# Gates by seven products and sums by accumulating transfers in a two-layer decoder trunk

## The chip, the cores and the metric

The kernel runs on one core of a Trainium2 chip. The metric is the device time of one execution in microseconds (us), the median of three runs. A core has five engines with a queue each: TensorE (PE), VectorE (DVE), ScalarE (ACT), GpSimd (POOL) and SyncE (SP, which here only issues transfers). DMA engines move data between HBM and the on-chip memory SBUF; matrix products are summed in PSUM banks of 128x512 fp32.

## The reference

One sequence of 256 tokens of width 1024 passes two layers. Layer 0 mixes tokens by gated linear attention (GLA), layer 1 by block attention (with 256 tokens this is plain causal attention). What the change touches is the output gate g of the GLA mixer and the feed-forward part (SwiGLU, hidden width 2816):

```python
def gla_mixer(x, w_in, w_gk, b_gk, norm_g, w_out):
    q, k, v, g, gk_low = split_cols(x @ w_in, GLA_COLS)
    ...
    o = chunk_gla(q, to_heads(k, GLA_HEADS), to_heads(v, GLA_HEADS), to_heads(log_a, GLA_HEADS))
    o = from_heads(rms_norm(o.astype(x.dtype), norm_g)) * jax.nn.silu(g)
    return o @ w_out

def swiglu_ffn(x, w_gu, w_down):
    gate, up = jnp.split(x @ w_gu, 2, axis=-1)
    return (jax.nn.silu(gate) * up) @ w_down
...
        x = layer_norm(DEEPNORM_ALPHA * x + y, ln_g[i, 0], ln_b[i, 0])
        x = layer_norm(DEEPNORM_ALPHA * x + swiglu_ffn(x, w_gu, w_down), ln_g[i, 1], ln_b[i, 1])
```

## The kernel before

**Precision.** Every fp32 operand of a large product is held as a high part (an ACT cast to fp32r, "h" at the end of its name) and a low part (a DVE subtraction, "l"). A product of 128 rows of contraction is three matmuls: high x high, low x high, high x low (`mm3`, lines 301 to 303; in the seven products lines 557, 559 and 560). A weight tile is 256 rows x 512 columns, loaded by SP as one raw tile of 128x1024 (512 KB), and split once into h and l (lines 265 and 266, in the feed-forward part 509 and 510).

**Tokens.** The 256 tokens are two blocks t of 128. The input x is transposed on PE into xT, with h and l. Contraction over 1024 is 8 slices of 128.

**GLA.** In turn: values v (first 512 columns), gate logits, keys, queries, scores (`sc`, and `scx` for the block below the diagonal, whose operand `kx` POOL copies, lines 794 and 797), the other half of v, then the output gates. `g_block` multiplies x by 512 gate columns for one token block: 8 slices x 3 matmuls, then a silu on ACT (line 878). The eight weight tiles wg00 to wg13 are split once and serve both token blocks. For each token block the scores times v give `o` (line 891), ACT sums its squares, POOL takes a power (`ss`, line 906), DVE forms `og` = o * ss * gate (line 916), PE transposes it (`trg`), and the output projection `wo` and the layer norm follow.

**Feed-forward.** Hidden columns are done in blocks: one plain block of 512, four of 512 by seven products (`seven`), one of 256. In `seven` the 2x2 product (two token blocks by gate and up columns, over two halves of the contraction) is formed from seven products instead of eight. Token sums s1 to s4 are made once (`x_sums`); weight sums are made in place: tile A takes A + X by DVE adds (line 577, 128x1024), three times two per block, and one sum X + weights is made by a transfer that POOL issues and that adds to what is in SBUF (line 583, two per block). The products go by the letters of their split tiles: A a00, B s1, C a01, D s2, E s4, F s3, G a11. From them come e1 and e2 (gate times up for the two token blocks; `e` in the rows, line 621 for e2's product), which PE transposes (line 316), and the rows of the previous block's `w_down` (d0, d1, ...) are multiplied in between.

**What sets the order.** All of this is recorded as operations for a planner (`Plan`), which hands them out greedily by its own costs per engine, by when operands are ready, by program order, and by whether one of 41 SBUF slots or of 8 PSUM banks is free. Each engine then runs its own list strictly in order. So an edit in one place moves instructions elsewhere.

Of the kernel before, what the change touches and what calls it, by code (L numbers as in the profile page):

```python
# [16 lines left out]
P = 128  # L17
# [174 lines left out]
def kernel(ctx, tc, x, positions, gla_w_in, gla_w_gk, gla_b_gk, gla_norm_g, gla_w_out,  # L192
# [44 lines left out]
    def act(n, fn, reads, writes, **kw):  # L237
        return pl.op("ACT", 0.16 + 0.00087 * n, fn, reads, writes, **kw)
# [71 lines left out]
    def transpose_split(src, dst, t, half, skey=None, dstf=None, dkey=None, n=4, keep=None):  # L310
# [157 lines left out]
    def ffn(i, xs, T, gb, dstT, last, x32):  # L468
# [73 lines left out]
        def seven(b, c0, pend, n=512, final=False):  # L542
# [37 lines left out]
            def add_dma(raws, kh, gu):  # L580
# [5 lines left out]
            ch = [load_unit(f"A{q}", unit(0, 0, q, c0, n), n) for q in range(units)]  # L586
            product(pa, "a00", [split_unit(f"A{q}", ch[q]) for q in range(units)], True, False)
            keep_(pa, e1, 0)
            add_to(ch, 0, 1)
            product(pc, "s1", [split_unit(f"B{q}", ch[q]) for q in range(units)], True, False)  # L590
            keep_(pc, e2, 0)
            add_dma(get(0, 1), 1, 1)
            r3 = get(1, 0)
            product(pb, "a01", [split_unit(f"C{q}", r3[q]) for q in range(units)], True, True)
            dve(n, lambda: nc.vector.tensor_tensor(out=e1.f[:, lo_], in0=pb.f[:, lo_], in1=e1.f[:, lo_], op=ALU.add),
                [pb, (e1, 0)], [(e1, 0)], urgent=True)
            act(n, lambda: nc.scalar.activation(e1.f[:, lo_], e1.f[:, lo_], AF.Silu), [(e1, 0)], [(e1, 0)],
                table="silu", urgent=True)
            add_to(ch, 1, 1)
            product(pa, "s2", [split_unit(f"D{q}", ch[q]) for q in range(units)], False, False)  # L600
            keep_(pa, e1, 1)
            r4 = get(1, 1)
            down_now(pend[:2], final)
            product(pc, "s4", [split_unit(f"E{q}", r4[q]) for q in range(units)], False, True)
# [65 lines left out]
    T0 = new_xT("xT0")  # L670
    load_x(0, 0, 2.9)
# [202 lines left out]
    def g_block(blk, t, ws):  # L874
        ps = pl.buf("acc", f"g{blk}{t}")
        act_block(ps, T0, ws, t)
        sl = slice(512 * blk, 512 * blk + 512)
        act(512, lambda: nc.scalar.activation(sg[t].f[:, sl], ps.f, AF.Silu), [ps], [(sg[t], blk)], table="silu")  # L878

    wgs = [load_cols("wg0", w0, G0), load_cols("wg1", w0, G0 + 512)]  # L880
    for t in range(2):
        if t == 1:
            v_block(1, 1, T0, wv1, v_sb)
        ob = [pl.buf("ps", f"o{t}{blk}") for blk in range(2)]
        for blk in range(2):
            def fo(blk=blk, t=t, ob=ob):
# [9 lines left out]
        for blk in range(2):  # L896
            def fsq(blk=blk, ob=ob, ss=ss, junk=junk):
                for j in range(2):
# [204 lines left out]
```

## Time and profile before

| | us |
|---|---|
| three runs: median (lowest to highest) | 581.41 (581.38 to 582.15) |
| the profiled execution | 580.57 |
| its span, first to last instruction | 578.8 |
| PE busy | 568.6 (98%) |
| DVE busy | 518.8 (90%) |
| ACT busy | 352.5 (61%) |
| POOL busy | 45.3 (8%) |

The page was made of one execution; its times count from the first instruction. Ends of matmuls are modelled, so how fast PE really goes is read from the starts of matmuls that follow each other. A wait is read in the list of who waited for whom, and at its place in the timeline.

### The profile page before, as it was taken

What the parts mean: (1) busy time and instruction counts of PE and PEld (TensorE: products, weight loads), DVE (VectorE), ACT (ScalarE), POOL (GpSimd) and SP (SyncE); (2) the same over time, 40 slices, a digit from 0 to 9 for tenths busy, and PEclk for the clock granted to TensorE, in tenths of its full rate; (3) what the DMA queues carried; (4) which work ended last, traced back from release to release, by engine and by line L of the source; (5) the groups of instructions that cost most, each with busy time, mean ns of one, the idle gap of its engine ahead of it and who ended that gap; (6) DMA issues with size and microseconds to landing.
All of it is one profiled execution on the core that took longest, in us unless ns stands there. A gap on an engine that the chain in (4) does not pass through costs nothing.

```text
span 578.8 us, 8048 instructions
## 1 busy us (share of the span) xinstructions
PE 568.6 (98%) x2980; PEld 485.6 (84%) x2980; DVE 518.8 (90%) x644; ACT 352.5 (61%) x469; POOL 45.3 (8%) x41
## 2 busy tenths in 40 slices
PE   9999999999999999999999999999999999999994
PEld 8898888888878888889889999888888788888883
DVE  5799467798999999999998789988989999999986
ACT  5696555346758586867454365734495767575720
POOL 1016000010010101000000000000101000010001
PEclk9999999999999999999999999999999999999999
DMA  9994286347896978869667445626867887877601
GB/s 289 352 327 145 76 265 244 110 129 234 265 217 224 257 236 239 209 215 285 215 212 228 160 144 179 208 74 218 215 203 221 213 286 176 307 179 236 183 1 72
DMA packets 57465, 119.38 MB, mean 206 GB/s; under 512 B 5265, under 2 KB 10801, under 8 KB 57426
## 3 DMA queue, kind: packets, MB, share of 16 engines
q1 hardware_dynamic: 51586, 108.84, 56.6%
q0 software_dynamic: 5408, 9.44, 10.1%
q10 hardware_dynamic: 432, 0.59, 0.3%
q8 instruction: 23, 0.38, 0.3%
q14 instruction: 16, 0.13, 0.1%
HBM read 117.81 MB, written 1.05 MB: 205 GB/s over the span
## 4 chain that ended last, share of the span: by engine, by line
PE 76%; DVE 9%; DMA 7%; ACT 3%; issue 3%; POOL 1%; DVEq 0%; ACTq 0%; SPq 0%
PE fy L303 6%; PE fy L301 6%; PE fy L302 6%; PE pa L560 4%; PE pa L559 4%; PE pa L557 4%; PE y L303 3%; PE y L302 3%; PE y L301 3%; DMA d0r<-in_ffn_w_down 2%; PE tr L316 2%; PE pc L557 2%; PE pc L560 2%; PE pc L559 2%; DVE A L577 2%
## 5 line engine op out<-in xcount | busy, mean ns | idle before, releaser
L577 DVE TENSOR_TENSOR A<-A,X 128x1024 f32<-128x1024 f32 x54 | 64.4, 1217 | 0.0
L583 POOL DMA_DIRECT2D X<-in_ffn_w_gu x18 | 22.2, 1261 | 261.2 <-PE fy L302 90.5
L325 ACT CAST xT<-tr 128x512 fp32r<-128x512 f32 x16 | 9.1, 590 | 31.1 <-PE tr L316 31.0
L372 POOL TENSOR_TENSOR st<-st,mhalf 128x1 f32<-128x1 f32 x8 | 7.6, 956 | 200.1 <-DVE st L370 200.1
L509 ACT CAST C0h<-X 128x1024 fp32r<-128x1024 f32 x10 | 10.5, 1051 | 16.8 <-DMA X<-in_ffn_w_gu 12.3
L509 ACT CAST B0h<-A 128x1024 fp32r<-128x1024 f32 x10 | 10.5, 1053 | 10.7 <-DVE A L577 10.7
L509 ACT CAST G0h<-A 128x1024 fp32r<-128x1024 f32 x10 | 10.5, 1052 | 6.8 <-DVE A L577 6.8
L509 ACT CAST A0h<-A 128x1024 fp32r<-128x1024 f32 x10 | 10.5, 1052 | 5.7 <-DMA A<-in_ffn_w_gu 5.5
L620 ACT ACTIVATE e<-pa 128x512 f32<-128x512 f32 (+1 forms) x10 | 5.5, 555 | 11.5 <-PE pa L560 11.5
L316 PEld LDWEIGHTS tr<-ident,e 128*128 128x128 f32 x72 | 8.7, 140 | 4.4 <-DVE e L621 1.9
L316 PE MATMUL tr<-ident,e 128*128 128x128 f32 x72 | 11.3, 274 | 1.0 <-DVE e L621 1.0
L509 ACT CAST D0h<-A 128x1024 fp32r<-128x1024 f32 x10 | 10.5, 1052 | 2.8 <-DVE A L577 2.8
L510 DVE TENSOR_TENSOR D0l<-A,D0h 128x1024 fp32r<-128x1024 f32 x10 | 12.2, 1219 | 0.0
L510 DVE TENSOR_TENSOR G0l<-A,G0h 128x1024 fp32r<-128x1024 f32 x10 | 12.2, 1218 | 0.0
L510 DVE TENSOR_TENSOR A0l<-A,A0h 128x1024 fp32r<-128x1024 f32 x10 | 12.2, 1218 | 0.0
L510 DVE TENSOR_TENSOR E0l<-X,E0h 128x1024 fp32r<-128x1024 f32 x10 | 12.2, 1218 | 0.0
L510 DVE TENSOR_TENSOR F0l<-X,F0h 128x1024 fp32r<-128x1024 f32 x10 | 12.2, 1218 | 0.0
L510 DVE TENSOR_TENSOR C0l<-X,C0h 128x1024 fp32r<-128x1024 f32 x10 | 12.2, 1217 | 0.0
L510 DVE TENSOR_TENSOR B0l<-A,B0h 128x1024 fp32r<-128x1024 f32 x10 | 12.2, 1216 | 0.0
L329 DVE TENSOR_TENSOR xT<-tr,xT 128x512 fp32r<-128x512 f32 x16 | 10.7, 684 | 1.5 <-ACT xT L325 0.9
L916 DVE SCALAR_TENSOR_TENSOR og<-o,ss,sg 128x256 f32<-128x256 f32 x8 | 3.6, 478 | 9.2 <-ACT sg L878 9.2
L364 DVE BATCH_NORM_STATS2 st<-r 128x6 f32<-128x512 f32 x16 | 11.1, 693 | 0.5
(1012 smaller groups left out, 2249.7 us busy)
## 6 DMA issues: line engine op xcount, KB each, us to landing
X<-in_ffn_w_gu SPq DMA_DIRECT2D x54, 512.0 KB, 4.8
A<-in_ffn_w_gu SPq DMA_DIRECT2D x18, 512.0 KB, 4.3
X<-in_ffn_w_gu POOLq DMA_DIRECT2D x18, 512.0 KB, 7.6
lng<-in_ln_g SPq DMA_DIRECT2D x4, 512.0 KB, 3.8
lnb<-in_ln_b SPq DMA_DIRECT2D x4, 512.0 KB, 5.4
x<-in_x SPq DMA_DIRECT2D x4, 256.0 KB, 3.8
fg00r<-in_ffn_w_gu SPq DMA_DIRECT2D x2, 512.0 KB, 6.6
fg01r<-in_ffn_w_gu SPq DMA_DIRECT2D x2, 512.0 KB, 7.0
```

Source lines behind the costliest of these rows:

```text
L301: nc.tensor.matmul(ps, lh, rh, start=start, stop=False)
L302: nc.tensor.matmul(ps, ll, rh, start=False, stop=False)
L303: nc.tensor.matmul(ps, lh, rl, start=False, stop=stop)
L316: nc.tensor.transpose(ps.f[:, j * P:(j + 1) * P], src.f[:, k * P:(k + 1) * P], ident.f)
L364: nc.vector.bn_stats(st.f[:, 6 * hf:6 * hf + 6], r.f[:, sl])
L509: act(1024, lambda: nc.scalar.copy(hi.r, raw.f), [raw], [hi])
L510: dve(1024, lambda: nc.vector.tensor_tensor(out=lo.r, in0=raw.f, in1=hi.f, op=ALU.subtract), [raw, hi], [lo])
L557: nc.tensor.matmul(ps.f[:, lo_], sh, wh.r[:, cs], start=first and q == 0 and j == 0, stop=False, skip_group_check=True)
L559: nc.tensor.matmul(ps.f[:, lo_], sl_, wh.r[:, cs], start=False, stop=False, skip_group_check=True)
L560: nc.tensor.matmul(ps.f[:, lo_], sh, wl.r[:, cs], start=False, stop=last_ and (q, j) == (units - 1, nk - 1), skip_group_check=True)
L577: dve(1024, lambda q=q, other=other: nc.vector.tensor_tensor(out=raws[q].f, in0=raws[q].f, in1=other.f, op=ALU.add), [raws[q], other], [ra ...
L583: nc.gpsimd.dma_start(uv(raws[q], n), unit(kh, gu, q, c0, n), accum_op=ALU.add)
```

## The change

**Gates.** `g_block` goes; `gate_seven` forms the gates of both token blocks by seven products of 4 slices each (84 matmuls for 96). For it the four transposed blocks of x are also kept as fp32 (`x32i`, `x32j`: four ACT copies, line 713 of the changed kernel) and `x_sums` is called for them. Six raw weight tiles (`gr000` to `gr111`) are loaded and split (`gwh`, `gwl`); the sums of weights are made by three pairs of accumulating transfers on POOL and one pair of DVE adds, and the sums are split again. Results are combined on DVE (line 971). `head_out` and `gated` are the two halves of the old loop over token blocks, and the second half of v for token block 1, the gating of block 0 and the head products of block 1 stand between the fifth and the sixth product.

**Feed-forward.** The third block (`b in (2,)`, the second by seven products) of each layer makes two of its four sums of weights by accumulating transfers more: A + (0,1) and X(1,1) + (0,1), in place of two DVE adds; one pair of plain loads goes; its products are called in another order.

```diff
@@ seven @@
+            if b in (2,):
+                ch = [load_unit(f"A{q}", unit(0, 0, q, c0, n), n) for q in range(units)]
+                product(pa, "a00", [split_unit(f"A{q}", ch[q]) for q in range(units)], True, False)
+                keep_(pa, e1, 0)
+                add_dma(ch, 0, 1)
+                product(pb, "a01", [split_unit(f"C{q}", raw) for q, raw in enumerate(get(1, 0))], True, True)
+                gate0()
+                r4 = get(1, 1)
+                product(pc, "s1", [split_unit(f"B{q}", ch[q]) for q in range(units)], True, False)
+                keep_(pc, e2, 0)
+                add_to(ch, 1, 1)
+                r4s = [split_unit(f"E{q}", r4[q]) for q in range(units)]
+                add_dma(r4, 0, 1)
+                have[0, 1] = r4
+                product(pa, "s2", [split_unit(f"D{q}", ch[q]) for q in range(units)], False, False)
+                keep_(pa, e1, 1)
+                product(pc, "s4", r4s, False, True)
+                down_now(pend[:2], final)
+            else:
...
@@ transposes of x @@
+        x_t[0, hf] = transpose_split(xs[0], T0, 0, hf, skey=hf)
...
+    for (t, hf), ps in x_t.items():
+        act(512, lambda t=t, hf=hf, ps=ps: nc.scalar.copy(xi32[t].f[:, 512 * hf:512 * hf + 512], ps.f),
+            [ps, wv0[3][0]], [(xi32[t], hf)])
...
@@ gates @@
-    wgs = [load_cols("wg0", w0, G0), load_cols("wg1", w0, G0 + 512)]
-    for t in range(2):
-        if t == 1:
-            v_block(1, 1, T0, wv1, v_sb)
...
-        for blk in range(2):
-            g_block(blk, t, wgs[blk])
...
+    def gate_seven(xsum, between):
...
+        def add_dma(raws, kh, cb):
+            for q in range(2):
+                dma_add(lambda q=q: nc.gpsimd.dma_start(uv(raws[q]), unit(kh, cb, q), accum_op=ALU.add), [raws[q]],
+                        [raws[q]])
...
+        w00 = load(0, 0)
+        product(pa, "a00", parts(w00), True, False)
+        keep_(pa, e1, 0)
+        add_dma(w00, 0, 1)
+        w10 = load(1, 0)
+        product(pb, "a01", parts(w10), True, True)
+        combine(e1, 0, pb, ALU.add)
+        silu(e1, 0)
+        w11 = load(1, 1)
+        product(pc, "s1", parts(w00), True, False)
+        keep_(pc, e2, 0)
+        add(w00, w11)
+        w11s = parts(w11)
+        add_dma(w11, 0, 1)
+        product(pa, "s2", parts(w00), False, False)
+        keep_(pa, e1, 1)
+        add_dma(w00, 1, 0)
+        product(pc, "s4", w11s, False, True)
+        combine(e1, 1, pc, ALU.subtract)
+        silu(e1, 1)
+        between()
+        product(pa, "s3", parts(w11), False, False)
+        combine(e2, 0, pa, ALU.subtract, flip=True)
+        silu(e2, 0)
+        product(pa, "a11", parts(w00), False, True)
+        silu(e2, 1, pa)
...
+    heads = {0: head_out(0)}
+    xsum = x_sums(xi32)
+
+    def between():
+        v_block(1, 1, T0, wv1, v_sb)
+        gated(0, *heads[0])
+        heads[1] = head_out(1)
+    gate_seven(xsum, between)
+    gated(1, *heads[1])
```

What the planner makes of it at three places. First DVE at the gates, before: low parts of gate weights (wg), of the projection (wo), and og of token block 0.

```order
L266 TENSOR_TENSOR wg10l_0_673<-wg10r_0_533,wg10h_0_616 128x1024
L266 TENSOR_TENSOR wg11l_0_677<-wg11r_0_551,wg11h_0_621 128x1024
L266 TENSOR_TENSOR wg12l_0_692<-wg12r_0_559,wg12h_0_634 128x1024
L266 TENSOR_TENSOR wg13l_0_700<-wg13r_0_591,wg13h_0_645 128x1024
L269 SCALAR_TENSOR_TENSOR wo0l_0_711<-wo0r_0_679,normg_67,wo0h_0_694 128x1024
L903 TENSOR_SCALAR ss_0_696<-ss_0_696 128x4
L916 SCALAR_TENSOR_TENSOR og0_0_742<-o00_0_681,ss_0_696,sg0_0_740 128x256 x2
L269 SCALAR_TENSOR_TENSOR wo1l_0_778<-wo1r_0_713,normg_67,wo1h_0_717 128x1024
L916 SCALAR_TENSOR_TENSOR og0_0_742<-o01_0_702,ss_0_696,sg0_0_740 128x256 x2
L933 TENSOR_TENSOR ogT_1_781<-trg_0_763,ogT_0_780 128x512
L269 SCALAR_TENSOR_TENSOR wo2l_0_798<-wo2r_0_776,normg_67,wo2h_0_785 128x1024
```

And of the change, from the last split of an untransferred tile on (gwl are low parts; gr000 and gr001 the tiles that transfers and adds change).

```order
L933 TENSOR_TENSOR gwl_0_727<-gr111_0_634,gwh_0_692 128x1024
L971 TENSOR_TENSOR sg0_0_724<-gb_0_717,sg0_0_724 128x512
L1042 SCALAR_TENSOR_TENSOR og0_0_751<-o00_0_680,ss_0_698,sg0_0_724 128x256 x2
L933 TENSOR_TENSOR gwl_0_762<-gr000_0_508,gwh_0_753 128x1024
L940 TENSOR_TENSOR gr000_0_508<-gr000_0_508,gr110_0_615 128x1024
L933 TENSOR_TENSOR gwl_0_789<-gr001_0_510,gwh_0_764 128x1024
L940 TENSOR_TENSOR gr001_0_510<-gr001_0_510,gr111_0_634 128x1024
L933 TENSOR_TENSOR gwl_0_808<-gr000_0_508,gwh_0_792 128x1024
L1059 TENSOR_TENSOR ogT_1_806<-trg_0_794,ogT_0_805 128x512
L933 TENSOR_TENSOR gwl_0_827<-gr001_0_510,gwh_0_810 128x1024
L269 SCALAR_TENSOR_TENSOR wo0l_0_839<-wo0r_0_784,normg_67,wo0h_0_786 128x1024
L269 SCALAR_TENSOR_TENSOR wo1l_0_854<-wo1r_0_819,normg_67,wo1h_0_842 128x1024
```

The gate weights' splits, once done before the first og, are now spread behind it, between adds, and the projection's splits come behind them.

POOL in the same part, before: copies for the scores, then the powers.

```order
L794 COPY kx_0_517<-ke_0_489 128x4x64
L797 COPY kx_0_517<-qd_0_595 128x4x64
L906 ISA
L906 TENSOR_TENSOR ss_0_696<-ss_0_696,mhalf_71 128x4
L906 TENSOR_TENSOR ss_0_846<-ss_0_846,mhalf_71 128x4
```

And of the change.

```order
L824 COPY kx_0_519<-qd_0_593 128x4x64
L945 DMA gr000_0_508<-in_gla_w_in 128x2x512
L945 DMA gr001_0_510<-in_gla_w_in 128x2x512
L1029 ISA
L1029 TENSOR_TENSOR ss_0_698<-ss_0_698,mhalf_71 128x4
L945 DMA gr110_0_615<-in_gla_w_in 128x2x512
L945 DMA gr111_0_634<-in_gla_w_in 128x2x512
L945 DMA gr000_0_508<-in_gla_w_in 128x2x512
L945 DMA gr001_0_510<-in_gla_w_in 128x2x512
L1029 TENSOR_TENSOR ss_0_822<-ss_0_822,mhalf_71 128x4
```

Six issues now stand between the copy of kx and the power of token block 1.

DVE between the first and the second block by seven products, layer 0, before: splits of the second block (B, C), two adds, then e2's product (line 621).

```order
L577 TENSOR_TENSOR A1_0_1443<-A1_0_1443,X1_0_1486 128x1024
L510 TENSOR_TENSOR B0l_0_1561<-A0_0_1436,B0h_0_1540 128x1024
L329 TENSOR_TENSOR hT1l_0_1572<-tr_0_1544,hT1h_0_1559 128x4x128
L510 TENSOR_TENSOR B1l_0_1574<-A1_0_1443,B1h_0_1564 128x1024
L510 TENSOR_TENSOR C0l_0_1582<-X0_0_1508,C0h_0_1520 128x1024
L510 TENSOR_TENSOR C1l_0_1594<-X1_0_1518,C1h_0_1530 128x1024
L577 TENSOR_TENSOR A0_0_1436<-A0_0_1436,X0_0_1555 128x1024
L577 TENSOR_TENSOR A1_0_1443<-A1_0_1443,X1_0_1557 128x1024
L621 TENSOR_TENSOR e2_0_1401<-e2_0_1401 128x512
L266 TENSOR_TENSOR d4l_0_1623<-d4r_0_1590,d4h_0_1592 128x1024
L510 TENSOR_TENSOR D0l_0_1632<-A0_0_1436,D0h_0_1614 128x1024
```

And of the change, where e2's product is line 644.

```order
L511 TENSOR_TENSOR A1l_0_1590<-A1_0_1503,A1h_0_1517 128x1024
L329 TENSOR_TENSOR hT1l_0_1600<-tr_0_1576,hT1h_0_1588 128x4x128
L511 TENSOR_TENSOR C0l_0_1603<-X0_0_1526,C0h_0_1541 128x1024
L511 TENSOR_TENSOR C1l_0_1611<-X1_0_1529,C1h_0_1556 128x1024
L511 TENSOR_TENSOR E0l_0_1621<-X0_0_1551,E0h_0_1598 128x1024
L511 TENSOR_TENSOR E1l_0_1631<-X1_0_1564,E1h_0_1619 128x1024
L511 TENSOR_TENSOR B0l_0_1633<-A0_0_1491,B0h_0_1623 128x1024
L578 TENSOR_TENSOR A0_0_1491<-A0_0_1491,X0_0_1551 128x1024
L644 TENSOR_TENSOR e2_0_1444<-e2_0_1444 128x512
L266 TENSOR_TENSOR d4l_0_1666<-d4r_0_1641,d4h_0_1643 128x1024
L511 TENSOR_TENSOR D0l_0_1675<-A0_0_1491,D0h_0_1657 128x1024
```

The two adds on A0 and A1 and the split of B1 that stood ahead of e2 have gone from there; the splits E0 and E1 and one add stand there now.

## Rows read from the trace of the kernel before

**Rows 1.** The page: busy time, share of the span and instructions of each engine

```profile
PE 568.6 (98%) x2980; PEld 485.6 (84%) x2980; DVE 518.8 (90%) x644; ACT 352.5 (61%) x469; POOL 45.3 (8%) x41
```

**Rows 2.** The waits of PE, all: for whom, us in total, times, longest

```profile
PE junk L651 <- DVE zeros L644: 1.1, 1, 1.1
PE tr L316 <- DVE e L621: 1.0, 2, 0.6
PE scx L824 <- POOL kx L797: 0.4, 1, 0.4
```

**Rows 3.** Timeline of PE, 9 to 19 us: start, us, engine, line, operation, out<-in

```profile
9.01 0.40 PE L301 MATMUL v<-wv00h,xT 128*128 128x512 f32 x1
...
19.00 0.39 PE L303 MATMUL v<-wv03l,xT 128*128 128x512 f32 x1
```

**Rows 4.** Stretches: busy us by engine (x instructions), PEclk, DMA share, GB/s

```profile
60.00:112.00 52.00, 52.00 (x241) 42.89 (x240) 33.02 (x44) 26.12 (x41) 3.02 (x3) 1.00 0.52 168
...
139.00:172.20 33.20, 32.61 (x147) 26.43 (x145) 31.76 (x32) 24.16 (x28) 2.41 (x2) 1.00 0.77 222
172.20:205.00 32.80, 32.80 (x151) 27.24 (x152) 32.77 (x33) 24.11 (x30) 2.44 (x2) 1.00 0.81 229
```

**Rows 5.** Timeline of PE, its last matmul

```profile
570.91 0.39 PE L303 MATMUL fy<-d21l,hT5h 128*128 128x512 f32 x1
```

**Rows 6.** Timeline of PE before the transposes of e, layers 0 and 1

```profile
171.24 0.39 PE L560 MATMUL pa<-A1l,xT 128*128 128x512 f32 x1
172.20 0.66 PE L316 MATMUL tr<-ident,e 128*128 128x128 f32 x4 [0.58 <-DVE e L621]
...
452.27 0.39 PE L560 MATMUL pa<-A1l,xT 128*128 128x512 f32 x1
453.12 0.66 PE L316 MATMUL tr<-ident,e 128*128 128x128 f32 x4 [0.45 <-DVE e L621]
```

**Rows 7.** Timeline of DVE at the same place, layer 0

```profile
166.93 1.21 DVE L510 TENSOR_TENSOR C0l<-X,C0h 128x1024 fp32r<-128x1024 f32 x1
168.06 1.21 DVE L510 TENSOR_TENSOR C1l<-X,C1h 128x1024 fp32r<-128x1024 f32 x1
169.20 2.35 DVE L577 TENSOR_TENSOR A<-A,X 128x1024 f32<-128x1024 f32 x2
171.47 0.68 DVE L621 TENSOR_TENSOR e<-e 128x512 f32<-128x512 f32 x1
172.07 1.21 DVE L266 TENSOR_TENSOR d4l<-d4r,d4h 128x1024 fp32r<-128x1024 f32 x1
```

**Rows 8.** The page: ACT's casts of 128x1024 and 128x512

```profile
L325 ACT CAST xT<-tr 128x512 fp32r<-128x512 f32 x16 | 9.1, 590 | 31.1 <-PE tr L316 31.0
...
L509 ACT CAST A0h<-A 128x1024 fp32r<-128x1024 f32 x10 | 10.5, 1052 | 5.7 <-DMA A<-in_ffn_w_gu 5.5
```

**Rows 9.** The chain that ended last: products with the scores

```profile
57.05 0.86 PE o L891 x4
...
76.14 3.45 PE o L891 x16
```

**Rows 10.** POOL's issues of accumulating transfers: ns min/median/max, and the landing

```profile
L583 POOL DMA_DIRECT2D X<-in_ffn_w_gu x18: 1203/1207/1392, 126.0 to 538.9; - x18
...
DMA to landing us min/median/max: 5.9/7.6/10.9
```

**Rows 11.** Timeline of DVE and of PE, 201 to 204 us

```profile
201.90 0.68 DVE L621 TENSOR_TENSOR e<-e 128x512 f32<-128x512 f32 x1
...
203.14 0.60 PE L316 MATMUL tr<-ident,e 128*128 128x128 f32 x4
```

**Rows 12.** Timeline of POOL's copies, 40 to 54 us

```profile
40.44 0.74 POOL L791 COPY kb<-ka 128x256 f32<-128x256 f32 x2 [37.68 <-DVE ka L767]
...
49.15 3.94 POOL L797 COPY kx<-qd 128x256 f32<-128x256 f32 x1 [0.99 <-DVE qd L775]
```

More of the change, by code (lines that the diff above doesn't have):

```diff
@@ L584, in add_dma @@
                     dma_add(f, [raws[q]], [raws[q]])
[L586 to L602, printed above, removed]
@@ L603, in seven, with gate0 @@
-            down_now(pend[:2], final)
-            product(pc, "s4", [split_unit(f"E{q}", r4[q]) for q in range(units)], False, True)
+            def gate0():
+                dve(n, lambda: nc.vector.tensor_tensor(out=e1.f[:, lo_], in0=pb.f[:, lo_], in1=e1.f[:, lo_], op=ALU.add),
+                    [pb, (e1, 0)], [(e1, 0)], urgent=True)
+                act(n, lambda: nc.scalar.activation(e1.f[:, lo_], e1.f[:, lo_], AF.Silu), [(e1, 0)], [(e1, 0)],
+                    table="silu", urgent=True)
@@ new lines, in seven @@
+            if b in (2,):
[17 more added lines that the diff above has]
+            else:
+                ch = [load_unit(f"A{q}", unit(0, 0, q, c0, n), n) for q in range(units)]
+                product(pa, "a00", [split_unit(f"A{q}", ch[q]) for q in range(units)], True, False)
+                keep_(pa, e1, 0)
+                add_to(ch, 0, 1)
+                product(pc, "s1", [split_unit(f"B{q}", ch[q]) for q in range(units)], True, False)
+                keep_(pc, e2, 0)
+                add_dma(get(0, 1), 1, 1)
+                r3 = get(1, 0)
+                product(pb, "a01", [split_unit(f"C{q}", r3[q]) for q in range(units)], True, True)
+                gate0()
+                add_to(ch, 1, 1)
+                product(pa, "s2", [split_unit(f"D{q}", ch[q]) for q in range(units)], False, False)
+                keep_(pa, e1, 1)
+                r4 = get(1, 1)
+                down_now(pend[:2], final)
+                product(pc, "s4", [split_unit(f"E{q}", r4[q]) for q in range(units)], False, True)
@@ L670 @@
     T0 = new_xT("xT0")
+    xi32, x_t = [S_("x32i"), S_("x32j")], {}
     load_x(0, 0, 2.9)
@@ L902 @@
             act(850, fsq, [ob[blk]], [(ss, blk), (junk, blk)])
-        dve(10, lambda ss=ss: nc.vector.tensor_scalar(out=ss.f[:, 4:8], in0=ss.f[:, 0:4], scalar1=1.0 / GLA_DV,
-                                                      scalar2=1e-6, op0=ALU.mult, op1=ALU.add),
+        dve(10, lambda: nc.vector.tensor_scalar(out=ss.f[:, 4:8], in0=ss.f[:, 0:4], scalar1=1.0 / GLA_DV,
+                                                scalar2=1e-6, op0=ALU.mult, op1=ALU.add),
             [(ss, 0), (ss, 1)], [(ss, 2)])
-        pl.op("POOL", 0.6, lambda ss=ss: nc.gpsimd.tensor_tensor(
+        pl.op("POOL", 0.6, lambda: nc.gpsimd.tensor_tensor(
@@ L907, with gated, fog @@
             out=ss.f[:, 8:12], in0=ss.f[:, 4:8], in1=mhalf.f.broadcast_to([P, 4]), op=ALU.pow),
             [(ss, 2), mhalf], [(ss, 3)])
+        return ob, ss
+    def gated(t, ob, ss):
         for blk in range(2):
-            g_block(blk, t, wgs[blk])
-        for blk in range(2):
+            part = blk ^ t
             for j in range(2):
-                def fog(blk=blk, j=j, t=t, ob=ob, ss=ss):
+                def fog(blk=blk, j=j, part=part):
                     h = 2 * blk + j
                     hs = slice(h * S, (h + 1) * S)
+                    gs = slice(512 * part + j * S, 512 * part + (j + 1) * S)
@@ L916, in fog @@
                     nc.vector.scalar_tensor_tensor(out=og[t].f[:, hs], in0=ob[blk].f[:, j * S:(j + 1) * S],
[L917 removed]
+                                                   scalar=ss.f[:, 8 + h:9 + h], in1=sg[t].f[:, gs],
                                                    op0=ALU.mult, op1=ALU.mult)
[L919 removed]
+                dve(256, fog, [ob[blk], (ss, 3), (sg[t], part)], [(og[t], (blk, j))], urgent=True)
```

85 lines of the change are left out of this document (70 added, 15 removed).

## The prediction

> **What bounds the kernel now.** I read the page's busy times first [rows 1]: PE 98%, DVE 90% of the span, so the question is whether PE ever waits for DVE. The list of what PE waited for answers it [rows 2]: three entries, 2.5 us in all, in 578.8 us. Its matmuls follow each other at their own pace: from the row at 9.01 to the one at 19.00 there are 44 steps of 128x512, (19.00 - 9.01) / 44 = 0.227 us each [rows 3], and PEclk is 1.00 in every stretch [rows 4], which is the upper of the two clock levels (2.4 GHz). So the end is set by the number of matmuls, plus about 6 us before PE is fed, plus the last layer norm after the last matmul at 570.91 [rows 5], plus the few places where PE does wait. Two of these are the same place in the two layers: in the first block of seven products PE has issued its last matmul at 171.24 and its transposes of e start at 172.20; at 452.27 and 453.12 in the second layer [rows 6]. A matmul takes 0.227, so the waits are 0.96 - 0.23 = 0.73 and 0.85 - 0.23 = 0.62, together 1.35 us. DVE is why: it multiplies e at 171.47, right behind two adds that started at 169.20 [rows 7], and from 139 to 205 it is busy 64.5 of 66 us [rows 4].
>
> **Gates of the linear attention: PE.** Before: 2 token blocks x 2 column blocks x 8 slices x 3 matmuls = 96. After: 7 products x 4 slices x 3 = 84. The other matmuls are the same in number and form. 12 x 0.227 = **2.72 us less**, if PE stays fed.
>
> **Gates: DVE and ACT.** 8 splits of 128x1024 become 14, and 2 DVE adds come in: +8 instructions. A row of that form is followed by the next after 1.13 us (166.93 to 168.06), one of 128x512 after 0.60 (171.47 to 172.07) [rows 7]. The sums of x are 4 adds and 4 low parts, the combinations of products 3 more: +11 of 128x512. 8 x 1.13 + 11 x 0.60 = 15.6 us more on DVE. From 60 to 112 us, between the gates and the end of the layer norm of the first token block, DVE is busy 33.02 of 52.00 [rows 4], so 19.0 idle, less the 2.7 by which PE gets shorter: 16.3 against 15.6. It fits as a total with 0.7 to spare, so the order decides. ACT gets 6 casts and 11 pieces of 128x512: at most 6 x 1.05 + 11 x 0.59 = 12.8 us [rows 8], against 52.00 - 26.12 = 25.9 idle in the same stretch [rows 4]. I cost it at nothing there; four of its copies (of the first transposes) stand ahead of the casts of the key weights, 4 x 0.59 = 2.4 us, and PE has the 44 matmuls of v above in front of those weights.
>
> **Gates: the order, walked by hand.** I added up DVE's new order from the step where it leaves the old one (qd done, 49.1 us) and PE's from its row at 57.05, with the 0.86 us of that row for each product with the scores in the first token block and 3.45 for both in the second [rows 9]. All that follows are estimates from these steps. An accumulating transfer takes 1.21 us of POOL to issue and lands 7.6 us after its issue began, 5.9 to 10.9 [rows 10]. The first pair can go when DVE has read the raw tiles (56.0 and 57.2) and lands near 63.7 and 65.0. DVE has by then 1.4 us more behind it than before and is next held by the first combination (PE's second product ends near 63.9), then silu and two products of og to 66.3; its split of the first transferred tile is done at 67.7, the second at 70.0. PE wants them at 69.6 and 72.9, since the 24 matmuls of v stand ahead. The sums of four blocks are split by 72.4 and 74.1, wanted at 74.3 and 75.6. The third pair of tiles lands by 78.7, is split by 83.7 and 85.0, wanted at 85.0 and 86.3. The last pair is issued behind it, lands by 81.7, is split by 86.8 and 88.0, wanted at 90.4 and 91.8. The normalised rows of the first token block are ready near 103.3, wanted at 104.9. The margins are 1.2 to 3.6 us, and none is negative: **no new wait of PE**. SP loses 8 loads here and gains 6; of what it queues behind them, the projection weights, each waits for a tile that PE or DVE frees before 82 us, some 6 us or more ahead of its use. Behind the POOL issues stand only the two powers of ss, wanted after 61 and 83.
>
> **The third feed-forward block of each layer.** Two DVE adds go (2 x 1.13 = 2.27 us per layer), two more accumulating transfers per layer come in, and the block's products stand in another order. No matmul goes. So the gain can only be a wait of PE that ends sooner, and that is the one at 171 and 452. From the first sum of x in a feed-forward part to the second product e of its first block of seven, DVE has 32 instructions of 128x1024 before and 31 after, in both layers, and 19 of 128x512 in both. So e is 1.13 us earlier against PE, and both waits are shorter than that: 0.73 and 0.62 go, **1.35 us less**. What is late next: the same product of the second block of seven, which DVE ends at 202.59 and PE takes at 203.14 (201.90 + 0.69 [rows 11]). PE comes 0.73 sooner and DVE 1.13 sooner, so the 0.55 grows to 0.95. The transfers of this block: the pair onto A is issued behind the splits of A, near 155 and 160, lands near 162 and 168, and is split at 166 and 173.7, PE wanting it at 171.6 and 175.7. The pair onto X lands near 175 and 183.5, wanted (after splits) at 185.2 and 189.7; the worst landing, 10.9, would make the last one 0.5 us late. I take nothing for it and keep 0.5 for the range. In all POOL issues 10 more transfers and SP 6 fewer: 4 x 0.52 = 2.1 MB more beside 119 MB; the 16 DMA engines are at most 0.81 busy in the feed-forward stretches shown [rows 4].
>
> **The sum.** The profiled execution took 580.57 us, 1.77 around its span of 578.8; the median of the three runs is 581.41, 0.84 above it. 580.57 - 2.72 - 1.35 = 576.5, and with 0.84 for the median **577.3**. About 0.2% (1.16 us) is what can be told from no change, so faster means under 580.25 and slower over 582.57.
>
> **Rivals.**
> *The block of sums gives nothing.* DVE's relief is spent by another order (its in-order queue now holds splits for the transfers ahead of e), and the waits at 171 and 452 stay. For it: DVE is full from 139 on, and the split of B ahead of e now waits for a transfer. Against: the count above, and 3 us between landing and split. 577.3 + 1.35 = 578.7.
> *The gates do not fit.* Transfers land at the long end, 10.9 instead of 7.6. The first pair then delays DVE by 1.4 us; with 0.7 to spare, 0.7 is left over at the layer norm, and the sums of x for the feed-forward part start late, so that the waits of the blocks come back too: 577.3 + 0.7 + 1.35 = 579.4. For it: margins of 1.2 us. Against: 7.6 is the middle of 18.
> *Slower: POOL's issues are held up by DVE.* A POOL copy takes 0.37 us at 40.44 (two in 0.74) and 3.94 at 49.15, where DVE subtracts without a pause [rows 12]. If the issues were stretched like that copy, 3.57 us each, then the two pairs that wait for each other at 69 to 82 us would bring the last tile 4 x 3.57 = 14.3 us later, against 8.0 us between its landing plus cast and split (83.8) and its use (91.8): PE waits 6.3 us, 577.3 + 6.3 = 583.6. It decides from 4 x d - 8.0 = 4.07, d = 3.0 us per issue. Against: the 18 issues of before took 1203 to 1392 ns [rows 10], and DVE was as busy there [rows 4].
> The Trainium skill, in "SBUF — State Buffer", section "SBUF: two separate sides", says that a VectorE instruction in a mode that takes both ports keeps GpSimd from writing the descriptors of a transfer that it issues, which is this rival's mechanism. By that rule each issue beside such an instruction would wait for its end, and the sum would be the slower one; the subtractions and adds beside these issues are two-input instructions, and the rows of the issues show no such hold.
> That the change does not do what it says can be left out: the count of matmuls is in its program.
>
> **How the numbers follow.** The forecast 0.55 (own range 576.3 to 578.2: the 0.4 us at the scx product [rows 2] could go too, and 0.5 for the late transfer and 0.4 for the spread of medians on the other side); no gain from the blocks 0.22; gates that do not fit 0.15; slower 0.08. The predicted time is the first, 577.3. The range 576.3 to 579.8 holds nearly all of the first, the second and most of the third. Faster 0.55 + 0.22 + 0.11 = 0.88, within 0.2% 0.05, slower 0.07.
>
> **What would show it.** In the profile after: 12 matmuls fewer; no row of PE waiting for DVE e; DVE idle between 60 and 112 down from 19 us to 1 or 2; the start of the first feed-forward matmul 2.7 us sooner; 28 POOL issues of 1.2 us. Wrong would be: PE waiting for gwl, for og or for xn (the gates do not fit), POOL issues over 3 us (the slower case), or the pause before the transposes of e still there.

## The result

The changed kernel takes 591.33 us against 581.57 in the same runs, a ratio of 1.0152 (95% interval 1.013 to 1.0174): slower by 9.8 us, where 577.3 was forecast. The profiled execution has a span of 590.0 us.

The busy times of the page, which answer to [rows 1]: PE has 12 matmuls fewer but was busy longer, and 97% instead of 98%.

```profile
PE 571.9 (97%) x2968; PEld 483.9 (82%) x2968; DVE 529.3 (90%) x659; ACT 362.4 (61%) x486; POOL 58.9 (10%) x51
```

What PE waited for, which answers to [rows 2] (columns: waiting engine, tile and line, what it waited for, us in total, times, longest): instead of three entries there are eleven, and the two large ones stand at the first product e of a block (line 634) and at the output projection (line 301).

```profile
PE tr L316 <- DVE e L634: 2.4, 2, 1.3
PE y L301 <- ACT ogT L1055: 2.2, 1, 2.2
PE ga L958 <- DVE gwl L933: 1.4, 2, 0.9
...
PE pc L558 <- ACT e L567: 0.9, 1, 0.9
PE pa L561 <- DVE D1l L511: 0.5, 1, 0.5
```

Where the time went is read from the starts of matmuls that both kernels have. The first one of the feed-forward part of layer 0 started at 114.46 us before, and now (timeline of PE):

```profile
120.78 0.40 PE L301 MATMUL pg<-fg00h,xT 128*128 128x512 f32 x1
```

Its counterpart in layer 1 starts at 403.32 instead of 394.82, and the last matmul is 10.8 us later. So +6.3 us belong to the gates, though they lost 2.7 us of matmuls, +2.2 to the feed-forward part of layer 0 and the mixer of layer 1, and +2.3 to the feed-forward part of layer 1.

**The gates.** The stretches of the changed kernel (columns as in [rows 4]: busy us of PE, PEld, DVE, ACT, POOL, then granted clock, DMA share, GB/s):

```profile
84.00:88.00 4.00, 3.99 (x20) 2.94 (x18) 2.14 (x5) 1.79 (x5) 0.17 (x1) 1.00 1.08 300
88.00:92.00 4.00, 1.19 (x4) 0.67 (x4) 0.87 (x1) 1.23 (x2) 1.77 (x1) 1.00 1.06 294
92.00:96.00 4.00, 3.65 (x8) 2.66 (x9) 1.82 (x2) 1.16 (x2) 0.00 (x0) 0.50 1.06 395
96.00:100.00 4.00, 4.00 (x13) 2.75 (x12) 3.08 (x4) 4.00 (x6) 0.00 (x0) 0.65 0.54 162
```

From 88 to 92 PE does 1.19 us of work; DVE, ACT and POOL are idle most of that time too; only the DMA engines are full (1.06). Behind the pause the granted clock is 0.50, the lower of its two levels (1.2 GHz), until about 98.7: the 14 matmuls that start from 92.35 to 98.69 take 6.62 us, where 14 x 0.227 = 3.18 are due. The pauses beyond a step, from the starts of matmuls, are 0.62 at 74.7, 1.09 at 87.6 and 2.40 at 89.7; with these 3.4 they make 7.5 of the 9.0 us lost here (6.3 later, and 2.7 of matmuls less). What ACT waits for in that stretch:

```profile
85.75 1.05 ACT L932 CAST gwh<-gr 128x1024 fp32r<-128x1024 f32 x1 [2.48 <-DMA gr<-in_gla_w_in]
...
90.77 1.04 ACT L932 CAST gwh<-gr 128x1024 fp32r<-128x1024 f32 x1 [3.23 <-DMA gr<-in_gla_w_in]
91.72 0.58 ACT L1055 CAST ogT<-trg 128x512 fp32r<-128x512 f32 x1
95.14 1.04 ACT L932 CAST gwh<-gr 128x1024 fp32r<-128x1024 f32 x1 [2.84 <-DMA gr<-in_gla_w_in]
```

The last gate tiles come in one by one, and ACT, which runs its list in order, stands before each of the last three; the cast of ogT, for which PE waits at 89.7, is behind the last but one. The issues of the transfers and their landing, which answer to [rows 10]:

```profile
L945 POOL DMA_DIRECT2D gr<-in_gla_w_in x6: 1203/1300/1543, 57.0 to 77.5; - x6
...
DMA to landing us min/median/max: 6.1/11.8/17.6
```

POOL needs 1.3 us for an issue, about as forecast (1.21). The landing takes 11.8 in the middle and 17.6 at most, where the prediction had 7.6 and 10.9.

**Why they land late** stands in the queue rows of the page (packets, MB, share of the time of 16 DMA engines; q1 holds the transfers of SP, q0 those of POOL, all of which accumulate in these two kernels). Before:

```profile
q1 hardware_dynamic: 51586, 108.84, 56.6%
q0 software_dynamic: 5408, 9.44, 10.1%
```

After:

```profile
q1 hardware_dynamic: 49954, 105.69, 53.6%
q0 software_dynamic: 8128, 14.68, 15.1%
```

Shares times span by MB: before, 0.566 x 578.8 / 108.84 = 3.0 us of all 16 engines per MB for a load, and 0.101 x 578.8 / 9.44 = 6.2 for an accumulating transfer. A tile of 0.524 MB is 1.6 us as a load and 3.2 us as an accumulating transfer. From 57 to 96 us the changed kernel asks for six such transfers (3.1 MB, 19.5 us) and the 16 loads that SP issues from 59.15 to 87.57 (8.4 MB, 25.2 us): 44.7 us of work in 39, as an estimate at the prices of the whole program. The stretch from 60 to 96 in the kernel before, and in the changed one:

```profile
60.00:96.00 36.00, 36.00 (x168) 29.90 (x167) 20.02 (x26) 21.45 (x34) 2.04 (x2) 1.00 0.67 219
```

```profile
60.00:96.00 36.00, 32.30 (x135) 25.20 (x134) 23.70 (x27) 20.84 (x34) 8.79 (x6) 0.94 1.06 310
```

The DMA share goes from 0.67 to 1.06 (full engines come out a little above 1 in this count). By queue, there in the changed kernel:

```profile
q1 hardware_dynamic: 2640, 8.07, 58.5%
q0 software_dynamic: 1591, 3.06, 46.9%
```

These two rows give lower prices for the full stretch, 0.585 x 36 / 8.07 = 2.6 us per MB for a load and 0.469 x 36 / 3.06 = 5.5 for an accumulating transfer, still one to two. At these the work is 39 us in 39: the engines are just full.

The Trainium skill, in "DMA: Bandwidth & Descriptors", section "Issuing engines are not separate DMA queues", says that transfers of SP, ACT and POOL run on the same 16 DMA engines and interleave. The rows agree: 58.5% and 46.9% fill one and the same set of engines.

### The profile page after: what moved, and what is told of

Same layout as the page of the kernel before. It is cut to its first block, busy times and chain, and to the rows that moved or that the text cites. A ratio compares the mean times of both kernels' runs of the same rounds, so it can differ in the third digit from the quotient of the medians.

```text
span 590.0 us, 8055 instructions
## 1 busy us (share of the span) xinstructions
PE 571.9 (97%) x2968; PEld 483.9 (82%) x2968; DVE 529.3 (90%) x659; ACT 362.4 (61%) x486; POOL 58.9 (10%) x51
## 3 DMA queue, kind: packets, MB, share of 16 engines
HBM read 119.90 MB, written 1.05 MB: 205 GB/s over the span
## 4 chain that ended last, share of the span: by engine, by line
PE 61%; DVE 5%; DMA 3%; issue 2%; ACT 2%; DVEq 0%; ACTq 0%
PE fy L301 6%; PE fy L302 6%; PE fy L303 6%; PE pa L561 4%; PE pa L558 4%; PE pa L560 4%; PE pc L558 2%; PE pc L561 2%; PE pc L560 2%; PE tr L316 2%; DMA d0r<-in_ffn_w_down 1%; PE mq L301 1%; PE mk L301 1%; PE mk L302 1%; PE mq L303 1%
## 5 line engine op out<-in xcount | busy, mean ns | idle before, releaser
L578 DVE TENSOR_TENSOR A<-A,X 128x1024 f32<-128x1024 f32 x50 | 60.0, 1217 | 0.0
L932 ACT CAST gwh<-gr 128x1024 fp32r<-128x1024 f32 x14 | 14.4, 1048 | 12.6 <-DMA gr<-in_gla_w_in 12.6
L933 DVE TENSOR_TENSOR gwl<-gr,gwh 128x1024 fp32r<-128x1024 f32 x14 | 16.8, 1214 | 4.6 <-ACT gwh L932 4.6
L567 ACT COPY e<-pa 128x512 f32<-128x512 f32 (+1 forms) x20 | 10.8, 539 | 2.5 <-PE pa L561 2.4
## 6 DMA issues: line engine op xcount, KB each, us to landing
gr<-in_gla_w_in POOLq DMA_DIRECT2D x6, 512.0 KB, 11.8
```

What stands on the lines that cost most here:

```text
L578: dve(1024, lambda q=q, other=other: nc.vector.tensor_tensor(out=raws[q].f, in0=raws[q].f, in1=other.f, op=ALU.add), [raws[q], other], [ra ...
L933: dve(1024, lambda raw=raw, hi=hi, lo=lo: nc.vector.tensor_tensor(out=lo.r, in0=raw.f, in1=hi.f, op=ALU.subtract), [raw, hi], [lo])
```

## The experiments

Theory D: accumulating transfers hold the DMA engines twice as long, and land too late. Its rivals at the gates: W, DVE and ACT have too much to do whenever the tiles land; L, the transfers have a long time of their own. All times are medians beside runs of the kernel before on the same chip (582.0 to 582.3). The profiled execution of before, 580.57, is at the fast end of its runs, so sizes below are taken from medians, and places from traces.

### One part at a time

The gates alone:

```diff
-            if b in (2,):
+            if b in ():
```

> The gates' part alone, the feed-forward blocks as before. In the changed kernel the first feed-forward matmul came at 120.78 us instead of 114.46 (+6.3), though 12 matmuls (2.7 us) are gone: about 9 us were lost at the gates. The rest of the loss lies in the two feed-forward parts (+1.2 and +2.5) and the mixer of layer 1 (+1.0). Theory 'two separate losses': 581.6 + 6.3 = 588 us (587 to 589). Rival 'one loss, the feed-forward part only inherits late data': 590 to 591, as the changed kernel.

Measured: 588.45 us, ratio 1.0116 (1.0095 to 1.0137). The feed-forward part alone is the kernel before with the new function `seven`, its gates untouched.

> The feed-forward part alone, the gates as before. Theory 'two separate losses': 581.6 + 1.2 + 2.5 = 585 us (584 to 586), with PE waiting for the first product e of the first block by seven products (1.2 to 1.5 us each) in both layers. Rival 'inherited': 580.3, the 1.35 us of the two waits of before gone, as forecast.

Measured: 583.52 us, ratio 1.0027 (1.0016 to 1.0038). Both parts cost time, the gates 6.3 us and the feed-forward part 1.4. That is 7.7 of the 9.8. The other 2 would come only with both together, but the three intervals are some 1.3, 1.2 and 0.6 us to either side, so this rest is hardly clear of nothing. Neither theory's number for the feed-forward part was met: it lies between them.

### Transfers that overwrite

In g_only:

```diff
-                dma_add(lambda q=q: nc.gpsimd.dma_start(uv(raws[q]), unit(kh, cb, q), accum_op=ALU.add), [raws[q]],
+                dma_add(lambda q=q: nc.gpsimd.dma_start(uv(raws[q]), unit(kh, cb, q)), [raws[q]],
```

> g_only, with the six transfers of the gates overwriting their tile instead of adding to it (what is left out: the sums of weights at these places; order, issues and bytes read are the same). Theory D: an accumulating transfer keeps the 16 DMA engines about twice as long as a load of the same size (3.0 against 1.6 us in the queues' rows of the changed kernel), from 60 to 96 us all engines are full, so the gates' tiles land up to 17.6 us after their issue. Then the landings fall to 6 to 9 us, the pause of PE at 89 to 92 and the fall of the clock go, and the time is 579 to 582. Rival W (DVE and ACT have too much work between 60 and 112, whenever the tiles land): 587 to 588, as g_only. Rival L (two dependent transfers have a fixed time of their own, whatever they do): 587 to 588 as well.

Measured: 580.74 us, ratio 0.9978 (0.9969 to 0.9988), 7.7 us less than g_only by nothing but the accumulation. (Its issues on POOL get shorter with it, 724 to 904 ns instead of 1203 to 1535; PE waits for no issue in either kernel.) The landing of the gate tiles in g_plain, and its row for the stretch in which the changed kernel paused:

```profile
DMA to landing us min/median/max: 4.3/5.3/8.8
```

```profile
88.00:92.00 4.00, 4.00 (x18) 3.22 (x18) 4.00 (x6) 3.13 (x5) 0.00 (x0) 1.00 1.05 386
```

The queue rows give the price once more, with the same MB in g_only and g_plain: 0.129 x 585.8 = 75.6 us for 24 accumulating transfers, 0.115 x 578.3 = 66.5 where six of them overwrite (g_only, then g_plain).

```profile
q0 software_dynamic: 7040, 12.58, 12.9%
```

```profile
q0 software_dynamic: 6272, 12.58, 11.5%
```

W falls: DVE and ACT do all their new work here and PE never waits for it at the gates. L falls as well: the landing is 5.3 us, and where the engines are less full an accumulating tile lands in 7.6 [rows 10], not in 17. The first feed-forward matmul of g_plain starts at 111.93 (timeline of PE):

```profile
111.93 0.40 PE L301 MATMUL pg<-fg00h,xT 128*128 128x512 f32 x1
```

That is 2.53 sooner than before, where 2.72 were forecast. So the walk by hand through DVE's and PE's order held where the tiles land in 5.3 us, sooner than its 7.6.

### Other traffic out of the way

In g_only, the four loads of layer-norm weights are called later in the program, `load_ln(0, 0)` between the matmuls of the output projection and its layer norm, and `load_ln(0, 1)` at the end of the feed-forward part:

```diff
-    gb = load_ln(0, 0)
+    gb = lambda: load_ln(0, 0)
...
+            if t == 0 and callable(gb):
+                gb = gb()
             xn.append(layer_norm(xo[t], y, gb, dstT, t, keep=keep))
```

> g_only, with the four loads of layer-norm weights (2.1 MB, 4 x 1.6 = 6.4 us of all 16 engines) taken out of the stretch from 59 to 96 us and put behind the projection's weights and the feed-forward part. Theory D: the last two gate tiles land 4 to 6 us sooner, the pause of PE at 89 to 92 (3.5 us) and most of the clock's fall behind it go: 581 to 584. Rivals W and L: the tiles are late for another reason, 587 to 588.

Measured: 584.80 us, ratio 1.0049 (1.0031 to 1.0066), 3.7 less than g_only, 0.8 above what D expected. The landing of the gate tiles, and the stretch of the pause, in g_ln_late:

```profile
DMA to landing us min/median/max: 6.3/10.2/12.5
```

```profile
88.00:92.00 4.00, 2.37 (x12) 1.59 (x10) 2.44 (x3) 3.60 (x4) 0.00 (x0) 1.00 1.09 292
```

The longest landing falls from 16.5 (g_only) to 12.5, PE pauses 1.6 us of these four where it was 2.5 in g_only, and the clock stays at 1.00, where g_only had 0.90 here and 0.67 in the next four. But the stretch did not get emptier, as the edit meant it to be (g_ln_late):

```profile
60.00:96.00 36.00, 34.13 (x153) 27.52 (x152) 28.67 (x34) 26.62 (x41) 8.87 (x6) 1.00 1.06 305
```

The DMA share is 1.06, against 1.05 in g_only: two of the four loads are still issued in it, at 76.14 and 76.56, and SP brings later loads forward. The last transfer is issued 3.2 us later (79.93 against 76.72), so the last gate tile is cast only 1 us sooner (92.31 against 93.26), not 4 to 6 us as D expected. So the 3.7 us are gained with another order of issues and of PE's work. Neither number was met, and this run alone does not tell D from its rivals; g_plain, above, and fewer transfers, below, do.

### Earlier issue

In g_only, `x_sums` is called behind the first two products, so that the splits of the first two tiles come first on DVE:

```diff
-    xsum = x_sums(xi32)
...
         silu(e1, 0)
+        xsum.update(x_sums(xi32))
         w11 = load(1, 1)
```

> g_only, with the sums of x for the gates formed behind the splits of the first two products instead of ahead of them, so that the first two accumulating transfers can be issued some 4 to 5 us sooner, at 50 to 53 us, where the DMA engines are nearly idle (busy share 0.01 to 0.02 from 48 to 56 in g_only). Theory D (the engines are full where the transfers run): the first pair lands within 8 us of its issue, each later pair moves forward by 5 us or more, the last tile is there at about 88 and not at 94, the pause of PE at 88 to 92 and the clock's fall go: 580 to 583 us, against 588.5. Rival (the last two pairs still meet the eight loads of the projection's weights, whatever the first does): 586 to 588.

Measured: 587.08 us, ratio 1.009 (1.0061 to 1.0119): the rival's number. The issues do move, from 57 to 53, but PE now waits elsewhere (waits of PE, then the timeline of ACT, then the landing of the gate tiles, all of g_xs):

```profile
PE o L1015 <- ACT v L428: 3.8, 1, 3.8
```

```profile
75.40 1.15 ACT L268 ACTIVATE wo3h<-wo3r,normg 128x1024 fp32r<-128x1024 f32 x1 [1.97 <-DMA wo3r<-in_gla_w_out]
...
78.92 1.15 ACT L268 ACTIVATE wo4h<-wo4r,normg 128x1024 fp32r<-128x1024 f32 x1 [1.89 <-DMA wo4r<-in_gla_w_out]
81.57 1.15 ACT L268 ACTIVATE wo5h<-wo5r,normg 128x1024 fp32r<-128x1024 f32 x1 [1.51 <-DMA wo5r<-in_gla_w_out]
...
83.14 0.56 ACT L428 COPY v<-v 128x512 f32<-128x512 f32 x1
```

```profile
DMA to landing us min/median/max: 6.0/11.5/21.8
```

ACT's copy of v, for which PE stands 3.8 us, is queued behind three casts of projection weights that wait for their loads. With four transfers issued from 67.8 to 73.5, the loads of SP are what comes late. So D's number was missed, and who suffers has changed; that the cause is the same is read from these rows of one execution (589.48 us, the slowest of four). Moving transfers inside a full stretch was no cure here.

### Fewer accumulating transfers

The last sum of the gates needs (1, 0), whose tiles are on the chip. In g_ln_late:

```diff
-        add_dma(w00, 1, 0)
+        add(w00, w10)
```

> g_ln_late, with the last sum of the gates' weights formed by two DVE adds from tiles on the chip, not by two accumulating transfers. Theory D: 2 x 0.52 MB x 6.0 us per MB = 6.3 us of all 16 DMA engines less before 96 us; the pauses of 1.8 and 0.5 us at 90 to 92 go: 581.5 to 583 us, against 584.8. Rival W: the two adds (2.3 us of DVE) come in PE's way and PE waits as long: 584 to 585.

Measured: 580.91 us, ratio 0.9991 (0.9977 to 1.0004), 3.9 less than g_ln_late and somewhat better than D expected. The gates lose nothing any more, with two adds more on DVE; the first feed-forward matmul (timeline of PE):

```profile
111.28 0.40 PE L301 MATMUL pg<-fg00h,xT 128*128 128x512 f32 x1
```

3.18 us sooner than before. The profiled execution (583.07 us, 2.2 above the median of this kernel) then loses it again at the layer norm of the feed-forward part, where PE waits 2.7 us (waits of PE):

```profile
PE tr L316 <- DVE xn L383: 2.7, 1, 2.7
```

Both edits together with the earlier issue:

> g_xs, and besides: the last sum of the gates by two DVE adds from tiles that are on the chip anyway, instead of two accumulating transfers (2 x 3.0 us of all DMA engines less, 2 x 1.13 us of DVE more), and the four loads of layer-norm weights moved out of the stretch. Theory D: all gate tiles land in time, the first feed-forward matmul comes at 112 us, as where the transfers only overwrite (111.93): 579 to 581 us, faster than the kernel before if the rest stays as there. Rival W (no room for two more adds on DVE): PE waits for them, 582 to 584.

Measured: 580.68 us, ratio 0.9973 (0.9961 to 0.9986), as D expected, though not by its mark: the first feed-forward matmul starts at 114.80, not at 112. The loss is early, at the matmul of the scores that waits for POOL's copy of kx (the 3.94 us of [rows 12]), and in the clock behind it (waits of PE, then stretches of g_xs_w10_ln):

```profile
PE scx L855 <- POOL kx L828: 0.8, 1, 0.8
```

```profile
52.00:56.00 4.00, 3.18 (x18) 2.85 (x18) 4.00 (x6) 0.59 (x1) 4.00 (x3) 0.74 0.14 17
56.00:60.00 4.00, 4.00 (x16) 3.27 (x15) 2.58 (x5) 1.51 (x3) 0.04 (x1) 0.83 1.06 177
```

So that copy goes to ACT:

```diff
-    gps(350, lambda: nc.gpsimd.tensor_copy(kxv()[:, 1, :, 0:CHUNK], ch(qd, 2)), [qd], [(kx, 3)])
+    act(256, lambda: nc.scalar.copy(kxv()[:, 1, :, 0:CHUNK], ch(qd, 2)), [qd], [(kx, 3)], urgent=True)
```

> g_xs_w10_ln, with the copy of a part of kx for the scores on ACT (idle there) and not on POOL (3.94 us beside DVE). PE's wait ahead of scx at 52.5 (0.98 us) and the clock of 0.74 to 0.83 behind it, from 52 to 60, go: 0.4 + 1.3 us less, 579 us (578.5 to 579.8), against 580.7. Rival (the clock falls for another reason than this wait, or ACT's copy comes late): 580.3 to 581.

Measured: 579.13 us, ratio 0.9952 (0.9939 to 0.9965): faster than both kernels, as expected. PE no longer waits for scx, and the clock is 1.00 (the same stretch of g_best):

```profile
52.00:60.00 8.00, 8.00 (x44) 6.94 (x43) 8.00 (x12) 4.42 (x13) 1.38 (x2) 1.00 0.80 132
```

The same copy on ACT in the kernel before tells how much of this is the gates':

> The kernel before, with only the copy of a part of kx on ACT instead of POOL. The wait ahead of scx in the profile of before is 0.60 us beyond the step and the clock stays at 1.00 behind it: 0.4 to 0.6 us less, 581.4 to 581.7 us, a ratio of 0.999. Then of the 2.9 us by which g_best beats the kernel before, some 2.4 belong to the gates. Rival (the copy alone is worth the 1.55 us between g_xs_w10_ln and g_best): 580.5.

Measured: 582.06 us, ratio 0.9995 (0.9986 to 1.0005). Alone it is worth nothing that can be told. So the 2.9 us by which g_best is faster belong to the gates by seven products with four accumulating transfers, and to the later loads of layer-norm weights; how much these loads would give in the kernel before was not tried.

### The feed-forward block

In f_only, only where b is 2:

```diff
-                        nc.gpsimd.dma_start(uv(raws[q], n), unit(kh, gu, q, c0, n), accum_op=ALU.add)
+                        nc.gpsimd.dma_start(uv(raws[q], n), unit(kh, gu, q, c0, n), **kw)
```

with `kw` empty in that block. Theory D against O, the new order of products. In the kernel before, one of this block's four sums is made by transfers already, X(0,1) + (1,1), so the change adds one pair per layer, not two. The edit makes both pairs overwrite, and f_plain has 14 accumulating transfers, fewer than the 18 of the kernel before.

> f_only, with the four new transfers of each third block's pairs overwriting their tile instead of adding (what is left out: these sums; order and bytes read are the same). Theory D (the new transfers keep the DMA engines busy, so that loads of the down weights and what is queued behind their casts on ACT come late): the waits of 0.9 and 1.4 us ahead of the product of E go, 581.0 to 581.8 us. Rival O (the new order of products: E's product follows D's at once, while its PSUM bank is still to be copied by ACT): they stay, 583 to 584, as f_only.

Measured: 580.89 us, ratio 0.9977 (0.9967 to 0.9987), 2.6 less than f_only. PE's waits in f_only, and in f_plain (lines 633 and 634 are the first product e of a block, line 643 of f_only is e2's):

```profile
PE pc L557 <- ACT e L566: 2.0, 2, 1.3
PE tr L316 <- DVE e L633: 1.2, 2, 0.8
...
PE tr L316 <- DVE e L643: 0.3, 1, 0.3
```

```profile
PE tr L316 <- DVE e L634: 1.7, 2, 0.9
```

The waits ahead of E's product go with the accumulation. Their way to PE, in f_only at the second layer (timeline of ACT, then of PE):

```profile
460.13 1.05 ACT L265 CAST d6h<-d6r 128x1024 fp32r<-128x1024 f32 x1 [3.38 <-DMA d6r<-in_ffn_w_down]
...
461.62 1.03 ACT L509 CAST D1h<-A 128x1024 fp32r<-128x1024 f32 x1
462.55 0.58 ACT L566 COPY e<-pc 128x512 f32<-128x512 f32 x1
```

```profile
461.54 0.39 PE L560 MATMUL pa<-D0l,s2hl 128*128 128x512 f32 x1
463.18 0.50 PE L557 MATMUL pc<-E0h,s4hl 128*128 128x512 f32 x1 [1.26 <-ACT e L566]
```

ACT waits 3.38 us for the down weights d6, the copy of the bank that E's product writes stands three places behind, and PE waits 1.26 for that. In f_plain the same cast still waits (timeline of ACT), and PE does not:

```profile
457.73 1.05 ACT L265 CAST d6h<-d6r 128x1024 fp32r<-128x1024 f32 x1 [1.91 <-DMA d6r<-in_ffn_w_down]
```

So part of ACT's wait comes with the new order, in which this cast stands early; the accumulation adds the part that reaches PE. The order alone:

```diff
+                down_now(pend[:2], final)
                 product(pc, "s4", r4s, False, True)
-                down_now(pend[:2], final)
```

> f_only, with the rows of the down projection multiplied between D's and E's product, as before the change, not behind both. Rival O: ACT has 24 matmuls (5.4 us) more to copy the bank of E's product, both waits ahead of it (0.9 and 1.4 us) go: 581.0 to 581.8 us. Theory D: the casts of the down weights are late, PE waits for them there instead, 583 to 584.

Measured: 582.91 us, ratio 1.001 (0.9998 to 1.0021). The number lies between O's and D's. The waits ahead of E's product are gone here too, but 0.6 us is all that it gives against f_only: smaller waits are there in their place, at D's product and at the second product e (waits of PE in f_down).

```profile
PE tr L316 <- DVE e L633: 1.0, 2, 0.7
...
PE pa L560 <- DVE D1l L510: 0.7, 2, 0.4
PE tr L316 <- DVE e L643: 0.6, 3, 0.3
```

So the order decides where PE waits, and taking the accumulation out gives more (2.6 us) than the old place of the down rows (0.6).

### Both parts, transfers overwriting

> The whole changed kernel, with its six new transfers at the gates and its eight in the feed-forward parts (two pairs in each third block) overwriting instead of adding (left out: these sums). Theory D, that the added time lies in the accumulating transfers: the gains seen apart add up, 582.0 - 1.3 (gates, transfers overwriting) - 1.1 (feed-forward part alike) = 579.6 us (578.8 to 580.4), against 591.3 of the changed kernel; PE does not pause at the gates and the clock stays at 1.00. Rival (the two parts together overfill DVE or SBUF, whatever the transfers take): 584 or more.

Measured: 579.86 us, ratio 0.9972 (0.9955 to 0.9989): 11.5 us less than the changed kernel, and the sum that D gave. Where the transfers overwrite, the two parts add up, with no rest such as the 2 us above; whether that rest is there at all, and by which wait, was not separated.

## Why the prediction was wrong, step by step

- **12 matmuls less, 2.72 us:** right. It was 2.53 (g_plain) and 3.18 us (g_w10_ln) at the first feed-forward matmul, where the tiles were in time; the second trace also lacks the wait of 0.4 us at scx that [rows 2] has.
- **DVE's 15.6 us fit into its idle 16.3:** right. Where the transfers overwrite, PE waits for nothing at the gates, nor does it in g_w10_ln with two adds more.
- **The landing, 7.6 us after the issue:** this is the step that failed. It was taken from [rows 10], from transfers that are issued in ones or twos some 30 us apart. Six within 21 us, beside SP's loads, took 6.1 to 17.6. The last tile was forecast by 81.7 and is cast at 95.14: its landing took 10.0 us longer than 7.6, and its issue, behind the tiles before it, came some 3.4 us later. All the margins of 1.2 to 3.6 us (1.3 to 3.8 by the times it gives) hung on that one number. The prediction added up DVE, ACT, POOL and SP for this stretch, but not the DMA engines; for them it gave 2.1 MB beside 119 MB in the whole program. The rows for the sum were on the page of before: 6.2 against 3.0 us per MB, which makes 44.7 us of work in 39.
- **The rival of gates that do not fit** had the mechanism, late landings, with a chance of 0.15. Its price of 0.7 + 1.35 us was wrong: it stopped at the longest landing of before, and counted the delay on DVE only. Its sign, PE waiting for gwl, is in the page (1.4 us). Measured were pauses of 4.1 us and 3.4 us by the clock, for which the prediction had no term.
- **The slower rival, POOL's issues held up by DVE:** did not happen. The six issues took 1203 to 1543 ns, far from the case, whether its 3.0 us are read as a whole issue (its sign) or as what is added to one (its sum, where 3.57 is 3.94 less 0.37); the side of the forecast was lost by another mechanism than the one that was named for it. The rule of the Trainium skill that stood beside it ("SBUF — State Buffer", section "SBUF: two separate sides") keeps GpSimd from writing descriptors while VectorE runs in a two-port mode. The subtractions and adds beside these issues are two-input instructions, and the rows show no hold beside them; the rule itself was not put to a test here.
- **The feed-forward block, 1.35 us less:** the two waits ahead of e2's transposes are gone in f_plain, and it takes 1.1 us less than the kernel before; as it also has fewer accumulating transfers, the relief of DVE alone is not shown as a number. With the accumulation the part costs 1.4 us: f_only is 2.6 us slower than f_plain, and the sign turned. The walk followed PE to the second product e and left out the first one of that block, where PE waits 1.7 us for the two layers in f_plain: DVE reaches it no sooner, since the two adds that went stand behind it. That wait does not need the change. The trace of b_kx, whose feed-forward part is that of before, has it at the same place (0.79 at 161.83 and 0.74 at 444.46), beside those at e2 (waits of PE in b_kx; line 611 is the first product e):

```profile
PE tr L316 <- DVE e L611: 1.5, 2, 0.8
PE tr L316 <- DVE e L621: 1.5, 3, 0.6
```

  So [rows 2], read from an execution of 580.57 us, the shortest of its kernel, need not show every wait that the kernel has: b_kx was profiled at 582.73.
- **The transfers of this block, 0.5 us late at the worst landing, taken as nothing:** their own landing was as forecast (7.6 in the middle and 11.0 at most in f_only). The loads of d6 beside them took 5.8 and 6.4 us instead of 5.2 and 4.9 in f_plain, and ACT stood in order behind those.

## What to carry to other kernels

Add up the DMA engines for the stretch in which transfers are added, as for any other engine: microseconds of the 16 engines per MB, by queue, from the page, times the MB of that stretch. Sums by accumulating transfers are not free when DVE is the fuller engine; each held the DMA engines here as long as two loads, and what suffers may be another load and, through an engine that casts in order, a matmul that has nothing to do with it. A landing time from a quiet stretch says nothing of a full one. And one trace is one execution: a wait that it lacks may be there in others of the same kernel.

## What the runs showed of the hardware

- An accumulating transfer of HBM to SBUF takes 6.0 to 6.2 us of all 16 DMA engines per MB, a load 2.9 to 3.0 (queue rows of the kernels before and after, g_only and f_only, over the whole program; 5.5 and 2.6 in the full stretch of the changed kernel).
- In the changed kernel PE starts no matmul from 89.73 to 92.35, and the lower clock follows for some 6.5 us. In g_ln_late PE was busy 2.37 of 4 us from 88 to 92, and the clock stayed at 1.00; in g_xs_w10_ln a wait of 0.8 us ahead of scx was followed by 0.74 and 0.83 in the next two stretches of 4 us. So what a wait costs by the clock could not be told from its length here.
